# A hybrid attention layer on one core: all first projections in a written order, first tokens without their shift, broadcast conditions, and 26 gate rows in the output projection

## The chip, the core and the metric

One Trainium2 chip; the kernel runs on one core of it. The metric is the device time of one execution in microseconds. The engines are named as in the profile: PE (TensorE, matrix products), DVE (VectorE), ACT (ScalarE), POOL (GpSimd), and SP, which here only issues DMA transfers. POOL can issue transfers too, on a queue of its own.

## The reference

One layer of a diffusion transformer over 512 latent tokens x and 256 context tokens (width 2048, float32), cut to what the first half computes:

```python
mod_x = silu(c) @ w_ada + b_ada          # 6 x 2048: sh1, s1, g1, sh2, s2, g2
mod_c = silu(c_ctx) @ w_ada + b_ada
h  = rmsnorm(x, norm1_w)   * (1 + s1)  + sh1
hc = rmsnorm(ctx, norm1_w) * (1 + s1c) + sh1c
p  = concat(h, hc) @ w_in                # q, k, v of 8 heads; latents c_q, c_kv; rotary key
o_da  = differential attention of 8 heads (two softmax maps each)
o_mla = latent attention of 8 heads (from rmsnorm(c_q), rmsnorm(c_kv))
x  = x + g1 * (concat(o_da, o_mla) @ w_o)
h2 = rmsnorm(x, norm2_w) * (1 + s2) + sh2
x  = rmsnorm(x + g2 * conv_ffn(h2), final_w)
```

sh1 and s1 are needed for both kinds of tokens; of g1, sh2, s2 and g2 only the latent half is used. Since h = u + sh1 with u the scaled and normed token, h @ w = u @ w + sh1 @ w: a shift can be left out of a product and its row of constants added afterwards.

## The kernel before

Tokens lie transposed: kt 0 to 15 are the sixteen pieces of 128 of the width, each 128 partitions by 512 latent (or 256 context) tokens. Every product is split in three: operands are a high float32r part and a low rest, and `mm3` issues high x high, high x low and low x high (L104 to L106). Making the two parts of a weight block is `split`: a copy on ACT (L80) and a subtraction on DVE (L81).

The order of instructions on each engine up to the feed-forward part comes from the framework's scheduler; only in the feed-forward part is it written by hand.

First stage. x and the context are squared and summed for the norm. c and c_ctx are loaded as rows, passed through silu on one partition and spread to all by products with ones (L199) and copies (L200): the tiles cb and ccb. `modulation(u)` makes scale and shift for kts 2u and 2u+1. The scale weights for both kts (adak, 2 MB) go through PE in products with 32 columns of conditions (L219), a copy of the result (row, L221) and a turn that puts it on partitions (L223). The shift weights of one kt (a row of `ada`, 1 MB, in two halves, L244) are multiplied with cb and ccb and summed on DVE for even kts (L251); for odd ones PE transposes them (L258), ACT copies (L259) and PE multiplies (L219). Then tokens: h = x * scale * 1/rms (L330), its high part with the shift (L332, ACT) and its low part (L333, DVE). With the split block of w_g0 (128 x 640) each kt feeds five latent and four context features, 15 matmuls of 512 columns and 12 of 256.

Second stage. ckv norm, keys of heads 0 and 1, query of head 0; features 0 to 6 (two blocks of weights each, `feature`); three features of c_q, without context; two halves of the values, eight blocks each (36 matmuls of 512). The keys, queries and values go to HBM (k_d, q0_d, v_d) as high and low parts. Beside this 48 rows for the gates and the second modulation are computed by `gemv`: a row of 1 MB loaded on SP's queue (L168) and one DVE instruction with an accumulator (L171). `next_gemv` takes the next rows, 32 to 79 here.

Then eight heads of differential attention (`da_head`: keys ks and klz are loaded at L527 and L528, scores at L482; head h's query is a feature computed just ahead), eight latent heads, the output projection (32 blocks, four groups g of eight kb, with 16 gate rows, L704), and the feed-forward part, half of the time.

Of the kernel before, what the change touches and what calls it, by code (L numbers as in the profile page):

```python
# [17 lines left out]
P = 128  # L18
D = 2048
KT = D // P  # L20
T = 512
# [31 lines left out]
def layer_kernel(ctx: ExitStack, tc: tile.TileContext, small, rope, c_row, cc_row, x_t, ctx_t, ada, ada_k,  # L53
# [33 lines left out]
    def wblock(src, cols=1024, pool=None):  # L87
        pool, full = (pool, cols) if pool else (wp, 1024)
        raw = pool.tile([P, full], F32, tag="wr", name=nm("wr"), bufs=3 if full == 1024 else 2)
        nc.sync.dma_start(raw[:, :cols], src)  # L90
        hi = pool.tile([P, full], F32R, tag="wh", name=nm("wh"), bufs=3)
        lo = pool.tile([P, full], F32R, tag="wl", name=nm("wl"), bufs=3)
        split(hi[:, :cols], lo[:, :cols], raw[:, :cols])
        return hi, lo
# [15 lines left out]
    sm.tile([P, 88], F32, name="edge")  # L110
# [55 lines left out]
    def gemv(pool, j, srcs, bufs=2):  # L166
        w = pool.tile([P, D], F32, tag="ada", name=nm("ada"), bufs=bufs)
        nc.sync.dma_start(w, ada[j])  # L168
# [11 lines left out]
    hcp = tc.alloc_tile_pool(name="hcp", bufs=17, side="right")  # L180
# [4 lines left out]
    st = tc.alloc_tile_pool(name="st", bufs=1, reuse_waits="tile")  # L185

    cb = st.tile([P, D], F32, name="cb")
    ccb = st.tile([P, D], F32, name="ccb")  # L190
    cpad = st.tile([P, KT, 32], F32, name="cpad")
    gp.memset(cpad, 0.0)
    sc.activation(cpad[:, :, 0:2], smt[:, OFF["cc"]:OFF["cc"] + 2 * KT].rearrange("p (k i) -> p k i", i=2), AF.Silu)
    for row, wide in ((c_row, cb), (cc_row, ccb)):
        nc.sync.dma_start(wide[0:1], row)
        sc.activation(wide[0:1], wide[0:1], AF.Silu)
        for j in range(0, D, 512):
            t = b_tile()
            pe.matmul(t, ones32[0:1], wide[0:1, j:j + 512], start=True, stop=True)  # L199
            ve.tensor_copy(wide[:, j:j + 512], t)  # L200
    exp_ln_tables()

    sel = sm.tile([P, 2], F32, name="sel")
    ve.tensor_tensor(sel, ident[:, 0:2], ident[:, 32:34], op=ALU.add)
    for j in (64, 96):
        ve.tensor_tensor(sel, sel, ident[:, j:j + 2], op=ALU.add)
    ve.tensor_scalar(out=b1, in0=smt[:, OFF["b_ada"] + 16:OFF["b_ada"] + 32], scalar1=1.0, scalar2=None, op0=ALU.add)


    g0b = [b_tile() for _ in range(4)]  # L210
    acc = g0b[3]

    def products(src, n):


        for j in range(4):
# [1057 lines left out]
```

## Time and profile before

| | us |
|---|---|
| median of 3 runs (lowest, highest) | 2451.57 (2449.83, 2454.16) |
| profiled execution, its own time | 2454.1 |
| its span, first to last instruction | 2451.9 |
| first stage, to the last matmul of the first projection | 0 to 182.9 |
| second stage | 186.7 to 477.9 |
| until the first score of the attention | 495.2 |
| output projection | 893 to 1062 |

The profiled execution lies 2.5 above the median. Times in the traces are from the first instruction on. "Busy" is the time in which an engine works on an instruction; a PE that is busy need not be on the path that sets the end. In rows such as `x48 | 112.8, 2349 | 50.5` the first number behind the bar is the group's busy time in us, the second the mean of one in ns, the third the engine's idle time ahead of them, with what ended it.

### The profile page before, as it was taken

The page shows a single profiled execution, that of the slowest core. Times are in us where ns is not written, and L with a number is a line of the kernel's source. Part 1 is how long each engine was busy: PE and PEld are TensorE (multiplying, and loading weights), DVE is VectorE, ACT ScalarE, POOL GpSimd, SP SyncE. Part 2 cuts the span into 40 slices and gives each one's busy share as a digit, 9 for nine tenths or more (in the row PEclk, how much of TensorE's full clock was granted, in tenths as well). Part 3 has the DMA queues.
Part 4 walks back from the last instruction along what each step waited for, and adds up shares of the span by engine and source line. Part 5 has one row for each costly group of instructions (what it writes and reads, how often), then busy time and mean ns, then how long its engine had stood idle before and what let it go on. Part 6 is the DMA issues. An engine that isn't in the chain of part 4 may idle for free.

```text
span 2451.9 us, 32940 instructions
## 1 busy us (share of the span) xinstructions
PE 2375.5 (97%) x12788; PEld 1988.9 (81%) x12788; DVE 1726.3 (70%) x2272; ACT 1102.5 (45%) x1666; POOL 242.1 (10%) x270
## 2 busy tenths in 40 slices
PE   7999999999999999999999999999999999999997
PEld 3778887877777778888888888888888888888887
DVE  4668785388868877377666666666666666666667
ACT  4342121155545542244545454545454545454553
POOL 0000000122100003100111111111111111111113
PEclk8999999999999999999999999999999999999999
DMA  7868898554411149423555655555555555555572
GB/s 276 283 228 297 321 340 289 189 181 137 141 59 44 44 159 337 152 85 112 134 141 135 141 135 141 134 142 134 140 135 143 133 143 133 144 132 142 133 213 78
DMA packets 130706, 403.31 MB, mean 164 GB/s; under 512 B 14323, under 2 KB 25075, under 8 KB 122099
## 3 DMA queue, kind: packets, MB, share of 16 engines
q1 hardware_dynamic: 104118, 350.87, 43.4%
q0 software_dynamic: 25280, 49.30, 11.5%
q8 instruction: 100, 1.64, 0.3%
q10 hardware_dynamic: 1152, 1.05, 0.1%
q14 instruction: 56, 0.46, 0.1%
HBM read 331.68 MB, written 69.48 MB: 164 GB/s over the span
## 4 chain that ended last, share of the span: by engine, by line
PE 84%; DVE 8%; ACT 3%; DMA 3%; issue 1%; POOL 1%; SPq 0%; DVEq 0%; ACTq 0%; POOLq 0%
PE y L973 12%; PE b L105 10%; PE b L104 10%; PE b L106 10%; PE z L973 6%; PE y L975 6%; PE z L975 3%; PE s L104 3%; PE s L105 3%; PE s L106 3%; PE s L482 3%; PE x L973 2%; DMA ada<-in_ada 2%; PE x L975 1%; PE f L104 1%
## 5 line engine op out<-in xcount | busy, mean ns | idle before, releaser
L104 PE MATMUL b<-ah,wh 128*128 128x512 f32 (+1 forms) x672 | 259.1, 386 | 0.0
L105 PE MATMUL b<-al,wh 128*128 128x512 f32 (+1 forms) x672 | 259.0, 385 | 0.0
L106 PE MATMUL b<-ah,wl 128*128 128x512 f32 (+1 forms) x672 | 258.0, 384 | 0.0
L994 POOL DMA_DIRECT2D x_d<-xs x160 | 139.7, 1003 | 1166.4 <-ACT xs L993 1164.3
L949 DVE TENSOR_TENSOR wl<-wr,wh 128x1024 fp32r<-128x1024 f32 x126 | 153.8, 1221 | 128.7 <-ACT wh L943 128.7
L949 DVE TENSOR_TENSOR wl<-rb,wh 128x1024 fp32r<-128x1024 f32 x124 | 151.2, 1220 | 128.0 <-ACT wh L943 128.0
L80 ACT CAST wh<-wr 128x1024 fp32r<-128x1024 f32 (+3 forms) x118 | 115.9, 982 | 259.0 <-PE b L105 68.3
L943 ACT CAST wh<-wr 128x1024 fp32r<-128x1024 f32 x126 | 132.3, 1050 | 206.3 <-PE b L105 100.7
L943 ACT CAST wh<-rb 128x1024 fp32r<-128x1024 f32 x124 | 130.2, 1051 | 190.0 <-PE b L105 112.5
L949 DVE TENSOR_TENSOR wl<-ws,wh 128x1024 fp32r<-128x1024 f32 x123 | 150.1, 1221 | 88.8 <-ACT wh L943 88.8
L81 DVE TENSOR_TENSOR wl<-wr,wh 128x1024 fp32r<-128x1024 f32 (+3 forms) x118 | 137.3, 1164 | 89.4 <-ACT wh L80 89.0
L171 DVE CUSTOM_DVE_ANT_0 ada<-ada,cb,smt 128x2048 f32<-128x2048 f32 x64 | 151.6, 2369 | 62.4 <-DMA ada<-in_ada 62.1
L943 ACT CAST wh<-ws 128x1024 fp32r<-128x1024 f32 x123 | 128.3, 1043 | 137.0 <-PE b L105 45.2
L106 PEld LDWEIGHTS b<-ah,wl 128*128 128x128 f32 x672 | 126.3, 188 | 25.6
L104 PEld LDWEIGHTS b<-ah,wh 128*128 128x128 f32 x672 | 126.6, 188 | 22.9
L105 PEld LDWEIGHTS b<-al,wh 128*128 128x128 f32 x672 | 126.6, 188 | 22.0
L104 PE MATMUL b<-a2k,wh 128*128 128x512 f32 (+1 forms) x352 | 133.1, 380 | 6.6 <-ACT a2k L756 5.0
L106 PE MATMUL b<-a2k,wl 128*128 128x512 f32 (+1 forms) x352 | 132.5, 376 | 0.0
L973 PE MATMUL y<-b2k,wh 128*128 128x512 f32 x410 | 106.9, 390 | 0.0
L484 DVE TENSOR_REDUCE m<-s 128x1 f32<-128x768 f32 x96 | 90.5, 949 | 15.3 <-PE s L482 14.9
L993 ACT ACTIVATE xs<-b,modx 128x512 f32<-128x512 f32 x160 | 101.0, 680 | 0.5 <-PE y L973 0.3
L973 PEld LDWEIGHTS y<-b2k,wh 128*128 128x128 f32 x410 | 77.0, 188 | 17.1
(471 smaller groups left out, 5937.4 us busy)
## 6 DMA issues: line engine op xcount, KB each, us to landing
ada<-in_ada SPq DMA_DIRECT2D x64, 1024.0 KB, 6.8
rb<-in_w_up SPq DMA_DIRECT2D x123, 512.0 KB, 4.4
wr<-in_w_dn SPq DMA_DIRECT2D x84, 512.0 KB, 4.3
x_d<-xs POOLq DMA_DIRECT2D x160, 256.0 KB, 6.0
wr<-in_w_up SPq DMA_DIRECT2D x53, 512.0 KB, 4.2
wr<-in_w_f SPq DMA_DIRECT2D x34, 512.0 KB, 5.9
adak<-in_ada_k SPq DMA_DIRECT2D x32, 512.0 KB, 6.2
ada<-in_ada SPq DMA_DIRECT2D x32, 512.0 KB, 6.6
```

Of the source, the lines that this page charges most:

```text
L80: sc.copy(dst_h, src)
L81: ve.tensor_tensor(dst_l, src, dst_h.bitcast(F32), op=ALU.subtract)
L104: pe.matmul(out, st[0], mv[0], start=start, stop=False, **kw)
L105: pe.matmul(out, st[0], mv[1], start=False, stop=False, **kw)
L106: pe.matmul(out, st[1], mv[0], start=False, stop=stop, **kw)
L171: ve.tensor_tensor_reduce(out=junk, in0=w, in1=vec, op0=ALU.mult, op1=ALU.add, scale=1.0, scalar=col("b_ada", j), accum_out=dst[:, j:j + 1])
L943: sc.copy(hi, raw)
L949: ve.tensor_tensor(lo, raw, hi.bitcast(F32), op=ALU.subtract)
L973: pe.matmul(o, w[j][0], hs[j], start=start and j == 0, stop=False, skip_group_check=True)
L975: pe.matmul(o[:, h0], w[j][1], hs[j][:, h0], start=False, stop=j == 7, skip_group_check=True)
L993: sc.mul(x, po, modx[:, 80 + dt:81 + dt])
L994: gp.dma_start(x1_d[dt], x, accum_op=ALU.add)
```

## The change

Both stages are written as straight code whose order on all five engines is the order of the program (`manual_schedule`). In words, part by part:

- SP loads x first, then scale weights for three passes, w_g0 and the context. cb and ccb are loaded to all 128 partitions (1 MB each) and passed through silu there; the products and copies that spread them are gone.
- Kts 0 to 7 enter the first projection and the first block of feature 0 without their shift (KA = 8). Shift rows come whole on POOL's queue into two buffers, in the order 8 to 15, 0 to 7, and all are summed on DVE; the transposes are gone. 23 of the 32 sums are ahead of feature 0, nine behind.
- `add_shift` adds the shift to the stored tokens of kts 0 to 7 on DVE and ACT beside the first values; the first half of the values takes its blocks in the order 4 to 7, 0 to 3.
- The row of constants that is missing (shift x w_g0, shift x first block of feature 0) is computed by `bias_products`: those weights are loaded once more on POOL's queue, into the rows' buffers, and multiplied on PE with the shifts padded to 32 columns. `with_bias` adds it on ACT to the outputs of the first projection and of feature 0, when they are used.
- Blocks come in the order: feature 0, values half 0, features 1 to 6 and c_q, values half 1. A block's raw weights have two buffers instead of three, its high and low part are made two blocks ahead (`step`). Keys 0 and 1 and the first query are made beside features 4 and 5, the norms beside feature 6 and the values.
- 64 `gemv` rows: 38 in the second stage on POOL's queue, 26 in the output projection on SP's (5 in group 0, 21 in groups 1 to 3).
- During the last value block the attention's key tiles are allocated, and head 0's keys and queries loaded; the values of the second half are split into twelve free tiles and put out on SP's queue.

The core of the diff:

```diff
+    KA, NU = 8, KT // 2
+    KB = ((4, 5, 6, 7, 0, 1, 2, 3), tuple(range(8)))
...
+    row_order = [*range(KA, KT), *range(KA)]
+    def row_load(kt):
+        rows[kt] = sp_.tile([P, D], F32, tag="ada", name=nm("ada"), bufs=2)
+        gp.dma_start(rows[kt], ada[kt])
+    def row_sums(count, upto=None):
...
+            if i and n_ < KT:
+                row_load(row_order[n_])
+    with tc.manual_schedule(engines=every):
...
+        for u in range(NU):
+            if u + 2 < NU:
+                scale_load(u + 2)
...
+            if u:
+                g0_mm(2 * u, (0, 1))
+            if u + 2 < NU:
+                scale_products(u + 2)
+            if u:
+                g0_mm(2 * u + 1, (0, 1))
+            if u + 1 < NU:
+                next_tokens(u)
+            if u + 2 < NU:
+                row = scale_row(u + 2)
+                scale_turn(u + 2, row)
...
+            elif u < NU - 1:
+                row_sums(3)
...
+    def step(block, *tasks):
+        i = len(steps)
+        block()
+        cast(i + 2)
+        for k, task in enumerate(tasks or [lambda: None]):
+            task()
+            if k == 0:
+                low(i + 2)
+                load(i + 4)
+        steps.append(i)
...
+        step(block(2, 0), feature_keys(1, gemvs(1)))
+        bias_products(0)
+        step(block(2, 1), gemvs(1), gemvs(1))
+        bias_products(1)
+        step(block(3, 0), feature_keys(2, gemvs(1)))
+        bias_products(2)
+        step(block(3, 1), gemvs(1))
+        bias_products(3)
+        bias_rows()
+        step(block(4, 0, bias_turn), feature_keys(3, gemvs(1)))
...
+        step(values(6), gemvs(1), gemvs(1))
+        sp_.release()
+        cbp.release()
+        block_ = values(7)
+        block_()
...
+        for i in range(2):
+            nc.sync.dma_start(qs0[i].bitcast(F32), q0_d[i])
+        keys0 = da_keys(0)
...
-            if g and kb % 4 != 3:
+            if kb != 7 if g else kb > 2:
                 next_gemv(wo, 1)
```

Where instructions now stand, at three places (the first on two engines). In these rows a2k are latent and c2k context tokens, wh and wl a block's high and low part, b_ and s_ tiles of PSUM.

PE inside the first projection, before: transposes of a shift row (ident, ada) and products with the copied result (wt) stand between the matmuls.

```order
L258 MATMUL b_189<-ident,ada_476 128x128 x8
L258 MATMUL b_189<-ident,ada_478 128x128 x4
L104 MATMUL s_428<-a2k_702,wh_472 128x512
L104 MATMUL s_429<-a2k_702,wh_472 128x512
L104 MATMUL b_186<-a2k_702,wh_472 128x512
L258 MATMUL b_189<-ident,ada_478 128x128 x4
L105 MATMUL s_428<-a2k_703,wh_472 128x512
L106 MATMUL s_428<-a2k_702,wl_473 128x512
L104 MATMUL b_187<-c2k_700,wh_472 128x256
L104 MATMUL s_428<-a2k_702,wh_472 128x512
L219 MATMUL b_189<-wt_480,cpad 32x128 x16
```

And now: between the matmuls of two kts only the scale products (adak) and their turn (sel, row).

```order
L285 MATMUL b_263<-adak_487,cpad 32x256 x2
L285 MATMUL b_263<-adak_489,cpad 32x256 x2
L285 MATMUL b_263<-adak_491,cpad 32x256 x2
L285 MATMUL b_263<-adak_493,cpad 32x256 x2
L285 MATMUL b_263<-adak_495,cpad 32x256 x2
L285 MATMUL b_263<-adak_497,cpad 32x256 x2
L285 MATMUL b_263<-adak_499,cpad 32x256 x2
L285 MATMUL b_263<-adak_501,cpad 32x256 x2
L296 MATMUL b_263<-sel,row_548 128x2 x2
L107 MATMUL b_260<-a2k_522,wh_536 128x512
L108 MATMUL b_260<-a2k_523,wh_536 128x512
L109 MATMUL b_260<-a2k_522,wl_537 128x512
```

The rows of L258 and their products are gone from PE; the products of a later pass stand in one piece ahead of the second kt.

DVE in one pass of the first projection, now: the scales of kts 8 and 9 (b_263), their tokens (h_, then the low parts a2k, c2k) and low parts of weights (wl), then the first of three sums over shift rows (a sum is two rows here, the second reads it out).

```order
L302 TENSOR_SCALAR a_91<-b_263,b_92,smt 128x2 x2
L381 SCALAR_TENSOR_TENSOR h_915<-a2k_185,a_91,rinv_269 128x512
L381 SCALAR_TENSOR_TENSOR h_915<-c2k_229,a_91,rinv_270 128x256
L381 SCALAR_TENSOR_TENSOR h_920<-a2k_187,a_91,rinv_269 128x512
L381 SCALAR_TENSOR_TENSOR h_920<-c2k_229,a_91,rinv_270 128x256
L244 SCALAR_TENSOR_TENSOR a2k_914<-h_915,modx,a2k_913 128x512
L244 SCALAR_TENSOR_TENSOR c2k_912<-h_915,modc,c2k_911 128x256
L389 TENSOR_TENSOR wl_928<-wr_837,wh_927 128x640
L244 SCALAR_TENSOR_TENSOR a2k_919<-h_920,modx,a2k_918 128x512
L244 SCALAR_TENSOR_TENSOR c2k_912<-h_920,modc,c2k_911 128x256
L389 TENSOR_TENSOR wl_936<-wr_839,wh_935 128x640
L260 ISA junk_943,modx<-ada_812,cb,smt 128x2048
```

Before, in the same place of the program, half of the rows were summed in pieces of 1024:

```order
L235 TENSOR_SCALAR a_91<-b_189,b_92,smt 128x2 x2
L330 SCALAR_TENSOR_TENSOR h_876<-a2k_220,a_91,rinv 128x512
L330 SCALAR_TENSOR_TENSOR h_912<-a2k_228,a_91,rinv 128x512
L330 SCALAR_TENSOR_TENSOR h_876<-c2k_222,a_91,rinv 128x256
L330 SCALAR_TENSOR_TENSOR h_912<-c2k_222,a_91,rinv 128x256
L251 ISA junk_636,modx<-ada_632,cb,smt 128x1024
L251 ISA modx 128x1
L81 TENSOR_TENSOR wl_645<-wr_642,wh_644 128x640
L251 ISA ada_632,modc<-ada_632,ccb,smt 128x1024
L251 ISA modc 128x1
L251 ISA junk_639,modx<-ada_634,cb,modx 128x1024
L251 ISA modx 128x1
```

What moved to DVE are the rows of the odd kts, and the sums of a row of kts 0 to 7 no longer stand ahead of that kt's tokens.

POOL beside features 1 to 3, now: the gate rows (ada) and the four loads for the missing constants (bw) share one queue.

```order
L171 DMA ada_2131<-in_ada 128x2048
L171 DMA ada_2198<-in_ada 128x2048
L647 MEMSET bias_2207 128x256
L656 DMA bw_2213<-in_w_g 128x640 x3
L171 DMA ada_2274<-in_ada 128x2048
L171 DMA ada_2280<-in_ada 128x2048
L656 DMA bw_2283<-in_w_g 128x640 x3
L171 DMA ada_2357<-in_ada 128x2048
L656 DMA bw_2366<-in_w_g 128x640 x2
L171 DMA ada_2424<-in_ada 128x2048
L664 DMA bw_2430<-in_w_f 128x1024
L171 DMA ada_2512<-in_ada 128x2048
```

Before, POOL's queue had nothing between the start and the second half of the values, where it put them out:

```order
L192 MEMSET cpad 128x512
masks.py:199 ISA
masks.py:199 AFFINE_SELECT ident<-ident 128x128
L470 DMA v_d_137<-kh_3769 128x4x128
L470 DMA v_d_137<-kl_3770 128x4x128
L470 DMA v_d_137<-kh_3775 128x4x128
L470 DMA v_d_137<-kl_3776 128x4x128
L470 DMA v_d_137<-kh_3781 128x4x128
```

The loads of gate rows moved from SP's queue to this one, the value puts from this one to SP's.

PE from the last value matmul into the attention, before: the query of head 1 (f_) stands ahead of the first score (L482).

```order
L105 MATMUL f_4000<-a2k_1599,wh_3765 128x512
L106 MATMUL f_4000<-a2k_1598,wl_3766 128x512
L104 MATMUL f_4000<-a2k_1636,wh_3765 128x512
L105 MATMUL f_4000<-a2k_1637,wh_3765 128x512
L106 MATMUL f_4000<-a2k_1636,wl_3766 128x512
L482 MATMUL s_3833<-ks_3825,qs_3821 128x512
L482 MATMUL s_3833<-klz_3815,qs_3821 128x512
L482 MATMUL s_3833<-ks_3825,qs_3821 128x256
```

Now the scores (L830) follow the last value block (L107 to L109):

```order
L107 MATMUL b_3159<-wh_3471,c2k_1273 128x512
L108 MATMUL b_3159<-wl_3472,c2k_1273 128x512
L109 MATMUL b_3159<-wh_3471,c2k_1274 128x512
L107 MATMUL b_3159<-wh_3471,c2k_1273 128x512
L108 MATMUL b_3159<-wl_3472,c2k_1273 128x512
L109 MATMUL b_3159<-wh_3471,c2k_1274 128x512
L830 MATMUL s_3647<-ks_3588,qs_3584 128x512
L830 MATMUL s_3647<-klz_3578,qs_3584 128x512
L830 MATMUL s_3647<-ks_3588,qs_3584 128x256
L830 MATMUL s_3647<-klz_3578,qs_3584 128x256
L830 MATMUL s_3656<-ks_3588,qs_3585 128x512
L107 MATMUL f_3813<-a2k_350,wh_3519 128x512
```

The query of head 1 has moved behind the first scores.

More of the change, by code (lines that the diff above doesn't have):

```diff
@@ L193, in layer_kernel @@
[L193 to L203, printed above, removed]
@@ L358, in next_block @@
         return wready.pop(0)
[L360 to L367 removed]
+    hx, hc, xs, cs, g0w, rows = [], [], [], [], [], {}
+    sel = sm.tile([P, 2], F32, name="sel")
```

742 lines of the change are left out of this document (496 added, 246 removed).

## Prediction

> **What bounds the kernel now.** I read the page first, then busy time by stretch, then the chain of waits and the groups of the first 190 us. The page (slices of 61 us):
>
> ```profile
> PE 2375.5 (97%) x12788; PEld 1988.9 (81%) x12788; DVE 1726.3 (70%) x2272; ACT 1102.5 (45%) x1666; POOL 242.1 (10%) x270
> ...
> PE   7999999999999999999999999999999999999997
> ...
> PEclk8999999999999999999999999999999999999999
> DMA  7868898554411149423555655555555555555572
> GB/s 276 283 228 297 321 340 289 189 181 137 141 59 44 44 159 337 152 85 112 134 141 135 141 135 141 134 142 134 140 135 143 133 143 133 144 132 142 133 213 78
> ```
>
> TensorE is busy throughout at the full granted clock except in the first slice; DVE (VectorE) has room. So only time in which TensorE idles, or does work that the change takes away, can be won. The stretches (entry; first projection; its end; features and values; way into the attention; output projection, and its part with gate rows):
>
> ```profile
> 0.00:75.20 75.20, 54.93 (x241) 29.82 (x241) 36.32 (x68) 31.65 (x58) 1.15 (x7) 0.91 0.73 264
> 75.20:182.90 107.70, 107.58 (x932) 83.71 (x932) 73.87 (x144) 43.20 (x85) 0.00 (x0) 1.00 0.77 263
> 182.90:186.70 3.80, 1.76 (x5) 0.68 (x4) 3.69 (x8) 2.23 (x4) 0.00 (x0) 1.00 0.03 12
> 186.70:477.90 291.20, 286.58 (x1393) 240.02 (x1394) 205.50 (x236) 62.03 (x78) 0.00 (x0) 0.99 0.81 291
> 477.90:495.20 17.30, 12.45 (x55) 9.96 (x54) 6.20 (x8) 4.99 (x8) 9.10 (x12) 0.92 0.81 278
> 893.00:1062.00 169.00, 168.43 (x734) 137.22 (x732) 93.92 (x86) 44.84 (x53) 29.03 (x27) 1.00 0.69 242
> 926.00:985.00 59.00, 59.00 (x262) 48.87 (x261) 43.73 (x38) 15.10 (x17) 18.00 (x13) 1.00 0.92 337
> ```
>
> TensorE works 55 of the first 75 us, nearly all of the next 108, 287 of 291 in the features, and all of the output projection. The entry and the projection are different cases: in the entry it waits; in the projection it is on the chain, but with shift work that after leaves out. From the chain of waits (start, length), and two places of the timeline of TensorE:
>
> ```profile
> 52.37 1.22 PE s L104 x2
> ...
> 75.20 0.73 PE s L104 x2
> ...
> 96.08 1.86 PE b L219 x32
> ...
> 98.73 0.37 PE b L223 x4
> ```
> ```profile
> 182.71 0.39 PE L106 MATMUL b<-a2k,wl 128*128 128x512 f32 x1
> ...
> 186.74 0.50 PE L104 MATMUL b<-a2k,wh 128*128 128x512 f32 x1 [1.57 <-ACT wh L80]
> ```
> ```profile
> 495.24 0.77 PE L482 MATMUL s<-ks,qs 128*128 128x512 f32 x1 [4.89 <-DMA ks<-k_d]
> ```
>
> Kt 0 starts at 52.37, kt 2 at 75.20, and the 14 kts from 2 to 15 end at 182.9. The second and third fence show the 3.8 us to feature 0, and the first score, which waited 4.89 us for a key transfer.
>
> **The change part by part.** All terms are against this execution: 2454.1 us, 2.5 above the median of the runs (2451.57).
>
> Entry, until kt 2's first matmul (75.2 now). After, x comes first, no shift row stands before kt 0 to 7, and c arrives by broadcast load. What must land before that matmul, from the DMA issues:
>
> ```profile
> x_d<-xs POOLq DMA_DIRECT2D x160, 256.0 KB, 6.0
> ...
> adak<-in_ada_k SPq DMA_DIRECT2D x32, 512.0 KB, 6.2
> ```
>
> One adak load is 512 KB, so a pass of two kts has 2.10 MB. x 4.19 MB (sixteen pieces of x_d's 256 KB) + three passes of adak 6.29 + four w_g0 rows 1.31 + context 2.10 + two broadcasts 2.10 + small 0.3 = 16.3 MB; the two rows that the POOL queue sends at once add some 1.6. At the best rate shown (337 GB/s, 926 to 985) 17.9 MB take 53 us, 3 more to the first landing, 1.9 for the products (row 96.08) that stand ahead of kt 2: 57, so **-18**. Bounds: 50, if the rows don't compete; 66, if 16.3 MB move at the entry's own 264 GB/s. I take the best rate, since the loads are queued without waits between them. Ends: -25 to -9. The products that spread c over partitions, and DVE's copies of them, go from a stretch in which TensorE is idle for 20 us; nothing is booked for them.
>
> First projection, kt 2 to 15. Its rows (75.2 to 182.9; x, mean ns behind the bar), and the pace of matmuls of both widths:
>
> ```profile
> L258 PE MATMUL b<-ident,ada 128*128 128x128 f32 x100 | 15.7, 280 | 0.0
> L259 ACT COPY wt<-b 128x512 f32<-128x512 f32 x26 | 15.2, 585 | 38.1 <-PE b L258 38.0
> ...
> L81 DVE TENSOR_TENSOR wl<-wr,wh 128x640 fp32r<-128x640 f32 x13 | 10.7, 820 | 0.1
> ...
> L333 DVE SCALAR_TENSOR_TENSOR a2k<-h,modx,a2k 128x512 fp32r<-128x512 f32 x14 | 10.5, 750 | 5.1 <-ACT a2k L332 5.1
> ...
> L330 DVE SCALAR_TENSOR_TENSOR h<-a2k,a,rinv 128x512 f32<-128x512 f32 x12 | 8.4, 744 | 0.0
> ...
> L219 PE MATMUL b<-wt,cpad 128*32 128x128 f32 x224 | 7.6, 276 | 0.0
> ...
> L333 DVE SCALAR_TENSOR_TENSOR c2k<-h,modc,c2k 128x256 fp32r<-128x256 f32 x14 | 6.7, 479 | 0.0
> ...
> L330 DVE SCALAR_TENSOR_TENSOR h<-c2k,a,rinv 128x256 f32<-128x256 f32 x12 | 5.2, 478 | 0.0
> ...
> L235 DVE TENSOR_SCALAR a<-b,b,smt 128x2 f32<-128x2 f32 x12 | 2.8, 275 | 8.3 <-PE b L223 8.3
> ```
> ```profile
> 195.80 0.40 PE L104 MATMUL b<-a2k,wh 128*128 128x512 f32 x1
> ...
> 196.85 0.40 PE L104 MATMUL b<-a2k,wh 128*128 128x512 f32 x1
> ```
>
> Six matmuls, three of 512 columns and three of 256, take 1.05 us: a kt with 15 and 12 takes 4.9. TensorE in a pass after: 9.8 + adak products 1.86 + turn 0.37 = 12.0. Gone are the transposes (L258, 15.7), the products with them (L219, 7.6) and the waits on ACT's copies (L259). On DVE a pass has 2 x (0.744 + 0.478 + 0.750 + 0.479 + 0.820) = 6.5 for tokens and low parts, three row sums, and 0.55 for the scales. A row sum and its read of the sum, and DVE's split of a block, from 186.7 to 477.9:
>
> ```profile
> L171 DVE CUSTOM_DVE_ANT_0 ada<-ada,cb,smt 128x2048 f32<-128x2048 f32 x48 | 112.8, 2349 | 50.5 <-DMA ada<-in_ada 50.2
> ...
> L81 DVE TENSOR_TENSOR wl<-wr,wh 128x1024 fp32r<-128x1024 f32 x38 | 46.4, 1221 | 26.9 <-ACT wh L80 26.7
> ...
> L171 DVE DVE_READ_ACCUMULATOR2_ANT modx<- 128x1 f32 x48 | 4.0, 82 | 0.0
> ```
>
> Three sums are 3 x 2.43 = 7.3, so DVE needs 14.4 a pass: it takes TensorE's place as the bound. DMA: 2.10 + 0.66 + 1.5 rows of 1.05 = 4.33 MB, 12.8 us at 337 GB/s. Five passes of 14.4; the sixth has no products, and its sums run beside the seventh, save one that kt 15 needs: 10.2; the seventh 9.8; 1 for the start: 93 against 107.7, **-14.7**. Ends: 87 (12.0 to 12.6 a pass) and 105 (17, second rival): -21 to -3.
>
> Its end. Feature 0's blocks are split beforehand; the norm sums and key work of 182.9 to 186.7 lie later, beside matmuls. 0.5 of 3.8 stays: **-3.3** (-3.8 to 0).
>
> Features and values. The matmuls are the same, and TensorE's 286.6 busy holds the norm sums too. Added on TensorE: correction products, 8 kts of 768 columns, 6144; a pass's adak products are 4096 columns in 1.86, so 2.8; six turns at 0.37 for two, 1.1. Then 290.5, and waits. DVE: 205.5 - 10 rows x 2.43 + the nine row sums left over from the first stage x 2.43 + 8 additions of shifts x (0.744 + 0.750 + 0.478 + 0.479) = 223, and, as an estimate, up to 17 of key and value splits that now stand in the stretches on both sides (where DVE shows 3.7 and 6.2 busy, so this is generous): 240 of 300, covered. The rows' loads, in this stage and in the output projection:
>
> ```profile
> DMA to landing us min/median/max: 4.8/6.8/9.5
> ```
> ```profile
> L171 DVE CUSTOM_DVE_ANT_0 ada<-ada,cb,smt x16: 2340/2352/3384, 901.2 to 984.4; 128x2048 f32<-128x2048 f32 x16
> ```
>
> With two buffers, and each next load behind the row's own sum on POOL's queue, a row comes each (6.8 + 0.75 + 2.43)/2 = 5.0 us (0.75 for issue, nearest row 0.866 below); from the second half of the first values on, four blocks of 8.2 want two rows each, one per 4.1. Two raw buffers for weights instead of three cost nothing while a 512 KB load lands in adak's 6.2 and a block lasts 8.2 or more. A lag of 0.9 x 8 = 7 us lies inside the two blocks (16 us) that are split ahead. It isn't covered where TensorE itself waits for a load behind those rows: the four correction loads use the rows' two buffers and queue. I put 6 us on the first and 4 on the second (a two-row cycle is 10 at most, and DVE's key work ahead of them uses part of it), none on the others, which stand a block later with one row between: 290.5 + 10 = 300.5, **+9**. Ends: 0 (the products fit into today's idle 4.6) and +30 (each of four points waits a full two-row cycle of 10 less 2.5).
>
> Into the attention. Keys and queries of head 0 are loaded during the last value block, so of 477.9 to 495.2 the 4.89 on ks go; head 1's query (part of its 12.45 busy) only moves behind the scores. **-5** (-6, if the 12.45 also run at the full clock instead of 0.92; -2, if the loads are late).
>
> Output projection. 26 rows instead of 16, 21 of them in 24 blocks. 32 blocks in 169.0 are 5.28 each, so a row per 6.0 us is asked; the sixteen rows from 901.2 to 984.4 came one per 5.55, beside a busy TensorE. **+1** (0 to +12).
>
> POOL issues 54 rows and the corrections. What one POOL issue takes now (DVE is busy 70% of the span, by the page):
>
> ```profile
> L994 POOL DMA_DIRECT2D x_d<-xs x160: 850/866/1232, 1194.7 to 2365.2; - x160
> ```
>
> 0.85 to 1.23, below a row's 5: hidden by POOL's empty queue (its next work is the 0-fills and key set-up before the attention). The Trainium skill ("SBUF — State Buffer", Who interferes with whom) speaks against this queue: a DMA issued from GpSimd waits for its descriptors while DVE runs a copy, cast or tensor_scalar in a two-port mode; a row sum is none of these, the nearest here are copies. This case's 160 issues show no such wait; by the rule the sum would rise as in the fifth rival. What is left (order inside the heads, MLA, FFN): 0, within 5.
>
> Sum: -18 - 14.7 - 3.3 + 9 - 5 + 1 = -31: 2423 for this execution, **2420** for the median.
>
> **The rivals.**
> 1. The fourth stage stretches: DVE in its written order comes late with low parts after the corrections. For it: DVE 240 of 300 in strict order, and row waits of 50.2 behind L171 now. Against: two blocks are split ahead. 20 more: 2440.
> 2. The projection waits for adak. Nine buffers hold one pass's eight, so the next eight start after the products (1.86) and then share the DMA with rows: 6.2 to land and 9 for 3 MB behind, 17 a pass. Five passes + 20 = 105: 12 more, 2432. Against: DMA has 13 of 14.4 to do.
> 3. Slower: rows on POOL's queue land late. 42 loads (38 rows, four corrections) through two buffers take 42 x (L + 2.8)/2; with L the time to land they pass 300 + 31 from L = 13 on; the gate rows bind the end, as the pool is released then. At 14 it is 353, and the kernel 2420 + 53 = 2473. For it: POOL's queue needs more engine time per MB:
>
> ```profile
> q1 hardware_dynamic: 104118, 350.87, 43.4%
> q0 software_dynamic: 25280, 49.30, 11.5%
> ```
>
> 0.23% against 0.12% per MB. Against: its transfers are 256 KB and less there, and land in 6.0, below the rows' 6.8 from SP.
> 4. The output projection becomes DMA-bound (share 0.92 with rows now), 10 more: 2430. Against: ten more rows are 31 us of transfers, and 0.31 of 169 is free.
> 5. Each POOL issue waits for the DVE instruction that runs, at most a sum's 2.35: L = 9.2, a row each 6.2. The eight rows in pairs then lag 17, one more than the cover; with the corrections' 2.35 each some 8 more: 2428. It is the mechanism of the skill's sentence above. Against: the issues took 0.87 at the median and 1.23 at most, with DVE at 70% over the span.
>
> **How the numbers follow.** About 0.2% (5 us) is what a measurement of this kernel tells from no change. Forecast 0.52, rivals 0.16, 0.11, 0.09, 0.08, 0.04. Of the first rival 0.03 eats the whole gain. Faster 0.88, same 0.03, slower 0.09. Range 2400 (entry and projection near their good ends, 13 together, and 7 of the features' 9 unneeded) to 2446 (rival 1 with most of 5).
>
> **What would show it.** Kt 0's first matmul near 30, kt 2's near 57; passes of 14 to 15 us with DVE over nine tenths; the last one ends near 150. TensorE waits for the two first correction loads and hardly otherwise; the first score right behind the last value matmul near 451; the output projection still near 169. Wrong: passes of 16 or more, low parts that TensorE waits for, rows landing over 9 us.

## Result, and the profile after

The changed kernel takes 2433.28 us (median of 4 runs, 2429.65 to 2436.97) against 2452.07 beside it: ratio 0.9924, 95% interval 0.9905 to 0.9942, so 19 us less. The forecast was 2420 in 2400 to 2446. The sign and the range held; the gain is three fifths of the forecast 32, and it came about otherwise than the sum said. Two terms were each far off, in opposite directions, and both lie outside the ends given for them. That the total still lies in the range is in part luck.

The page of the profile after (its span is 2430.2, so 21.7 below the span before; slices of 61 us):

```profile
PE 2332.7 (96%) x12408; PEld 1962.5 (81%) x12408; DVE 1779.8 (73%) x2305; ACT 1102.3 (45%) x1660; POOL 273.2 (11%) x324
...
PE   5989799999999999989999999999999999999997
...
PEclk9999899999999999999999999999999999999999
DMA  9865877854411159723546555555555555555572
```

The first slice now moves more, and a dip stands in TensorE's fifth slice, where the kernel before had none. Busy time by stretch (entry to kt 2; first projection; features and values; to the first score; output projection):

```profile
0.00:55.50 55.50, 31.08 (x174) 19.40 (x175) 31.49 (x65) 27.32 (x48) 2.65 (x10) 0.91 0.93 352
55.50:138.60 83.10, 81.46 (x561) 66.84 (x561) 78.85 (x109) 28.41 (x47) 5.27 (x10) 1.00 0.80 282
138.60:464.10 325.50, 300.79 (x1467) 248.46 (x1465) 240.11 (x296) 85.81 (x126) 30.79 (x57) 0.96 0.73 257
464.10:466.00 1.90, 0.38 (x3) 0.04 (x1) 1.64 (x3) 0.70 (x2) 0.00 (x0) 1.00 1.06 239
874.00:1042.00 168.00, 167.43 (x732) 137.02 (x731) 119.04 (x106) 45.00 (x53) 32.65 (x27) 1.00 0.82 306
```

Kt 2 starts at 55.5 instead of 75.2, the first projection ends at 138.6 instead of 182.9: 44 us are won there. The third row is the reader's main one: 325.5 us, to the start of the last value matmul, for a stage that took 293.1 before (186.7 to 479.8, where the last value matmul starts there, and not to the 477.9 that the prediction took as the end). TensorE is busy in 300.8 of them at a mean clock of 0.96. What it waited for between 100 and 300:

```profile
PE s L107 <- DVE kl L81: 7.8, 1, 7.8
PE b L109 <- DVE wl L213: 7.2, 1, 7.2
PE b L660 <- DVE a L1064: 6.7, 1, 6.7
PE b L108 <- DVE wl L213: 2.5, 1, 2.5
```

Four waits, 24 us, and each has a place. The 7.2 is feature 0's first block: its low part stands behind five row sums in DVE's written order.

```profile
131.94 0.82 DVE L389 TENSOR_TENSOR wl<-wr,wh 128x640 fp32r<-128x640 f32 x1
132.69 2.34 DVE L260 CUSTOM_DVE_ANT_0 junk<-ada,cb,smt 128x2048 bf16<-128x2048 f32 x1
...
135.07 2.35 DVE L260 CUSTOM_DVE_ANT_0 ada<-ada,ccb,smt 128x2048 f32<-128x2048 f32 x1
...
137.35 2.35 DVE L260 CUSTOM_DVE_ANT_0 junk<-ada,cb,smt 128x2048 bf16<-128x2048 f32 x1
...
139.74 2.35 DVE L260 CUSTOM_DVE_ANT_0 ada<-ada,ccb,smt 128x2048 f32<-128x2048 f32 x1
...
142.70 2.35 DVE L260 CUSTOM_DVE_ANT_0 junk<-ada,cb,smt 128x2048 bf16<-128x2048 f32 x1 [0.60 <-DMA ada<-in_ada]
...
144.98 1.22 DVE L213 TENSOR_TENSOR wl<-wr,wh 128x1024 fp32r<-128x1024 f32 x1
```

TensorE had finished the first projection at 138.7 and could go on at 146.2. The 2.5 is the same at 197, behind additions of shifts. The 7.8 (at 250) is a PSUM tile that isn't free, because the splits of the first half of the values wait for tiles that are still being put out; the 6.7 (at 268) is the first correction product, whose padded shifts (the copies `bias`) and weights stand behind these splits, the keys of feature 1 and two row sums. (The tile `a` that the wait names is a small unrelated operation, the last one on DVE ahead of the product.)

```profile
252.26 0.69 DVE L81 TENSOR_TENSOR kl<-s,kh 128x512 fp32r<-128x512 f32 x1 [5.06 <-DMA v_d<-kl]
...
257.48 0.69 DVE L81 TENSOR_TENSOR kl<-s,kh 128x512 fp32r<-128x512 f32 x1 [4.40 <-DMA v_d<-kl]
...
274.92 0.17 DVE L649 COPY bias<-modx 128x8 f32<-128x8 f32 x1
```

**What a long wait costs on top.** TensorE's busy time and granted clock (the last but two columns) around the first wait:

```profile
131.00:138.60 7.60, 7.60 (x45) 6.66 (x44) 7.43 (x8) 2.54 (x4) 1.06 (x2) 1.00 0.63 217
142.00:146.20 4.20, 0.00 (x0) 0.00 (x0) 3.60 (x6) 1.50 (x4) 0.53 (x1) 0.72 0.60 193
146.20:149.20 3.00, 2.94 (x7) 2.39 (x8) 3.00 (x4) 0.00 (x0) 0.43 (x1) 0.50 0.77 259
149.20:152.20 3.00, 3.00 (x11) 2.36 (x11) 3.00 (x4) 1.05 (x1) 0.09 (x1) 0.75 0.69 229
152.20:155.00 2.80, 2.80 (x20) 2.55 (x19) 2.80 (x3) 0.00 (x0) 0.53 (x1) 1.00 0.81 316
```

After 7 idle us TensorE runs at half clock for 3 us and regains the full clock by 152. Between 146.2 and 152.2 that is 0.5 x 3 + 0.25 x 3 = 2.3 us of clock lost. The Trainium skill ("TensorE: Matmul & The Clock Gate", What's actually happening) says that the throttled clock is the default state and that some 3.4 us of sustained work releases it; the trace agrees, with 3 to 6. The prediction had no term for this.

Where the 32 us of the longer stage are: the four waits 24, half clock behind the three long ones 3 x 2.3 = 7, the correction products about 8 (starts to starts), less the one wait of 4.6 and its half clock (0.50 and 0.52 for 3 us each, so 2.9) that the kernel before had here. That makes 31 to 32; about 1 of it is counted twice, since the first correction products run at half clock.

### The profile page after: what moved, and what is told of

It reads as the page before. It is cut to its first block, busy times and chain, and to the rows that moved or that the text cites. A ratio compares the mean times of both kernels' runs of the same rounds, so it can differ in the third digit from the quotient of the medians.

```text
span 2430.2 us, 32271 instructions
## 1 busy us (share of the span) xinstructions
PE 2332.7 (96%) x12408; PEld 1962.5 (81%) x12408; DVE 1779.8 (73%) x2305; ACT 1102.3 (45%) x1660; POOL 273.2 (11%) x324
## 4 chain that ended last, share of the span: by engine, by line
PE 78%; DVE 8%; issue 7%; DMA 3%; ACT 3%; POOL 1%; SPq 0%; DVEq 0%; POOLq 0%; ACTq 0%
PE y L1314 12%; PE b L108 9%; PE b L107 9%; PE b L109 9%; PE z L1314 6%; PE y L1316 6%; PE z L1316 3%; PE s L830 3%; PE x L1314 2%; PE s L108 2%; PE s L109 2%; PE s L107 2%; PE f L107 1%; PE x L1316 1%; PE pt L842 1%
## 5 line engine op out<-in xcount | busy, mean ns | idle before, releaser
L107 PE MATMUL b<-ah,wh 128*128 128x512 f32 (+1 forms) x672 | 259.1, 386 | 0.0
L109 PE MATMUL b<-ah,wl 128*128 128x512 f32 (+1 forms) x672 | 258.0, 384 | 0.0
L1284 ACT CAST wh<-wr 128x1024 fp32r<-128x1024 f32 x126 | 132.3, 1050 | 206.1 <-PE b L108 100.4
L109 PEld LDWEIGHTS b<-ah,wl 128*128 128x128 f32 x672 | 126.3, 188 | 25.6
L107 PEld LDWEIGHTS b<-ah,wh 128*128 128x128 f32 x672 | 126.6, 188 | 23.0
L107 PE MATMUL b<-a2k,wh 128*128 128x512 f32 (+1 forms) x352 | 136.5, 390 | 7.1 <-ACT a2k L1097 5.1
L109 PE MATMUL b<-a2k,wl 128*128 128x512 f32 (+1 forms) x352 | 134.3, 382 | 7.2 <-DVE wl L213 7.2
L80 ACT CAST wh<-wr 128x1024 fp32r<-128x1024 f32 (+2 forms) x64 | 64.3, 1005 | 135.0 <-PE b L108 42.9
L210 ACT CAST wh<-wr 128x1024 fp32r<-128x1024 f32 x38 | 39.9, 1049 | 141.5 <-PE s L108 46.1
L81 DVE TENSOR_TENSOR wl<-wr,wh 128x1024 fp32r<-128x1024 f32 (+2 forms) x64 | 78.3, 1223 | 32.3 <-ACT wh L80 31.9
```

What stands on the lines that cost most here:

```text
L81: ve.tensor_tensor(dst_l, src, dst_h.bitcast(F32), op=ALU.subtract)
L107: pe.matmul(out, st[0], mv[0], start=start, stop=False, **kw)
L109: pe.matmul(out, st[1], mv[0], start=False, stop=stop, **kw)
L1284: sc.copy(hi, raw)
```

## Experiments

All kernels but one start from the changed one and are compared by ratio to the kernel before, run beside them on the same chip. Times in the table are from each trace; "last row" is the start of the last gate row of the stage on DVE. In the kernel before, and in the one made from it, the query of head 1 stands ahead of the first score, so their first scores don't compare with the others'.

| | median us | ratio (95%) | last row | last value matmul | first score |
|---|---|---|---|---|---|
| kernel before | | 1 | 446.6 | 479.8 | 495.2 |
| changed kernel | 2433.3 | 0.9924 (0.9905 to 0.9942) | 455.9 | 464.1 | 466.0 |
| low parts first | 2438.1 | 0.9948 (0.9931 to 0.9966) | 459.9 | 466.6 | 469.8 |
| third pair of put tiles | 2437.2 | 0.9938 (0.9919 to 0.9958) | 459.1 | 467.2 | 468.8 |
| constants early | 2435.6 | 0.9928 (0.9911 to 0.9946) | 455.2 | 463.9 | 465.0 |
| these three | 2433.3 | 0.9929 (0.9905 to 0.9953) | 457.3 | 466.2 | 467.1 |
| seven rows later | 2434.6 | 0.9940 (0.9925 to 0.9955) | 454.2 | 453.6 | 464.3 |
| rows later and the three | 2437.6 | 0.9959 (0.9943 to 0.9976) | 454.0 | 453.0 | 466.0 |
| puts of 2 KB | 2433.0 | 0.9933 (0.9918 to 0.9947) | 453.7 | 462.8 | 463.8 |
| 16 gate rows at the end | 2471.1 | 1.0084 (1.0065 to 1.0102) | 486.6 | 483.9 | 496.3 |
| rows spaced | 2429.9 | 0.9920 (0.9903 to 0.9936) | 437.8 | 459.1 | 459.4 |
| spaced, and order | 2419.5 | 0.9883 (0.9867 to 0.9899) | 434.4 | 456.0 | 456.2 |
| before, 26 rows | 2447.2 | 0.9992 (0.9983 to 1.0002) | 392.6 | 474.3 | 489.5 |
| kts 0 to 3 unshifted | 2434.9 | 0.9945 (0.9924 to 0.9966) | 452.4 | 462.0 | 464.3 |

### Taking the waits away one by one

Low parts first:

```diff
                 for i in range(2):
                     cast(i)
-                    row_sums(2)
                     low(i)
                     load(i + 2)
-                row_sums(1)
+                row_sums(5)
...
+        early = i < 10
+        if early:
+            low(i + 2)
+            load(i + 4)
         for k, task in enumerate(tasks or [lambda: None]):
             task()
-            if k == 0:
+            if k == 0 and not early:
```

> Base: the changed kernel (span 2430.2, median 2433.3), in which TensorE waits 7.4 us for the low part of feature 0's first block and 2.7 for one of the first values, both behind row sums or shift additions in DVE's written order, and runs 4 to 5 us at half clock behind the long wait. Here the low parts of the first twelve blocks stand ahead of the sums of their step. Theory A (each wait is only a matter of order and is worth itself plus about 2.2 of half clock): both waits fall to under 2.5 together, last value matmul 10 earlier, median near 2423. Theory B (DVE is full until the shifts are added at 207, so what is not waited for here is waited for at the next low part): less than 4 gained, 2430.

```profile
PE b L663 <- DVE a L1067: 10.7, 1, 10.7
PE s L107 <- DVE kl L81: 8.7, 1, 8.7
PE b L107 <- ACT wh L210: 2.8, 1, 2.8
PE b L108 <- DVE wl L213: 2.0, 4, 0.8
```

The wait at 139 fell to 1.5 and the values began 7 us earlier (157.9 instead of 164.7), but the wait for the PSUM tile grew to 8.7 and the one for the constants to 10.7. The last value matmul came no earlier (466.6 instead of 464.1). Theory B's outcome, at other places than it named.

Third pair of put tiles:

```diff
-            return [lambda t=t: put_value(0, v0, t) for t in ts]
+            return [lambda t=t, k=k: put_value(0, v0, t, [rtmp(F32R), rtmp(F32R)] if k % 3 == 2 else None)
+                    for k, t in enumerate(ts)]
```

> Base: the changed kernel, in which TensorE waits 8.0 us ahead of feature 2's context half for a PSUM tile, while the splits of the first half of the values wait on DVE for their two pairs of tiles to be put out (5.1 and 4.4 us on v_d<-kl). Here every third put uses the two free tiles of the rotary work, so three pairs rotate. Theory A: the 8.0 and the half clock behind it (2.2) go, and the wait of 6.9 for the constants, which stands behind the same splits on DVE, shrinks by 3 or more: 11 to 14 less, median near 2420. Theory B (the puts land as slowly whatever the tile, because 512-byte pieces share the DMA with rows and weights): the wait only moves to the next pair or to the keys, 3 less, 2430.

```profile
PE b L660 <- DVE a L1065: 15.6, 1, 15.6
```

The wait of 7.8 is gone, and the next one has grown from 6.7 to 15.6: theory B again.

Constants early (padding behind the first half of the values, first load one step earlier):

```diff
+        bias_prep()
         step(block(1, 0), a, b, gemvs(1), c)
...
+        bias_load(0)
         step(block(2, 0), feature_keys(1, gemvs(1)))
         bias_products(0)
```

> Base: the changed kernel, in which TensorE waits 6.9 us for the first correction product. Here the shifts are padded (two copies on DVE) right behind the first half of the values, and the first correction load stands one step earlier on POOL's queue; products stay where they are. Theory A (the wait is for the two DVE copies and for a load that stand behind splits and a row sum): the 6.9 and the half clock behind it go, 9 less, median near 2424. Theory B (what is late is the transfer itself, behind the rows that share two buffers): the gate rows come later instead, or the second load waits: 2 less, 2431.

The wait went from 6.7 on DVE to 5.0 on the transfer of the weights, and the stage ended where it did (463.9). All three together:

> All three edits at once on the changed kernel. Theory A: the gains add, 10 + 10 + 9 = 29 less, median near 2404, stage from feature 0 to the last value matmul near 297 instead of 325. Theory B (DVE's total of 240 and the rows' cycle of 5 us are the limit, and waits only move): less than half of it, 2420 or more.

Theory A is refuted: 466.2, with waits of 7.3 and 8.0 between 246 and 272. What is saved before 246 is lost in the same 40 us.

### Is it the transfers?

The changed kernel's windows show a trough and a burst (the last two columns are the DMA share and GB/s):

```profile
180.00:190.00 10.00, 10.00 (x46) 8.29 (x45) 6.35 (x11) 4.21 (x7) 0.00 (x0) 1.00 0.24 83
190.00:200.00 10.00, 7.70 (x34) 6.03 (x33) 6.68 (x12) 3.91 (x6) 0.00 (x0) 1.00 0.00 0
200.00:210.00 10.00, 9.76 (x43) 7.96 (x44) 7.26 (x11) 3.42 (x5) 0.00 (x0) 1.00 0.23 64
210.00:290.00 80.00, 65.00 (x316) 52.63 (x315) 54.15 (x74) 12.68 (x17) 10.94 (x21) 0.89 0.90 308
```

From 180 to 210 hardly anything moves: DVE adds shifts, no row is asked for beyond the two that lie ready, and the next weights wait for buffers. Then puts, rows, corrections and weights come at once. Seven rows moved out of the burst, to seven steps from feature 5 to the second value block:

```diff
-                [gemvs(1), gemvs(1)], [gemvs(1), gemvs(1)], [gemvs(1), gemvs(1)], [gemvs(1), gemvs(1)])
+                [gemvs(1)], [gemvs(1)], [gemvs(1)], [gemvs(1)])
...
-        step(block(1, 1), d, gemvs(1), e_, f_, gemvs(1))
+        step(block(1, 1), d, e_, f_)
...
-        step(values(1), gemvs(1))
+        step(values(1), gemvs(1), gemvs(1))
```

> Base: the changed kernel. Its DMA is idle from 185 to 205 and busy 0.83 to 1.00 from 210 to 290, where twelve gate rows, the puts of the first half of the values, 3.1 MB of correction weights and the split blocks' weights fall together. Here seven gate rows move from that stretch to steps between features 5 and the second value block (38 rows in all as before). Theory C (that burst of DMA is the bound until 290, the waits of 8.0 and 6.9 are where TensorE meets it): 7 MB less are 20 us of DMA, both waits shrink to under 4 together, stage 12 to 15 shorter, median near 2420. Theory D (the two pairs of put tiles and DVE's written order set these waits, whatever the DMA does): within 3 us of 2433.

> The three edits of order (low parts first, third pair of put tiles, constants early) and the seven rows moved later, together. Theory C: what the three edits of order won before 210 is no longer given back at 246 to 290: 20 to 25 less than the changed kernel, median near 2411. Theory D: as with the three alone, 2433.

Theory C was right about TensorE: both waits are gone, and the last value matmul is at 453.6 and 453.0 instead of 464.1. A row that moves takes its sum on DVE with it, but DVE was busy in only 54 of the 80 us from 210 to 290, and it is the transfers that changed: the puts of the first half of the values land in 4.9 us at the median instead of 8.3. Theory C's times are refuted: the first kernel is no faster, and the second looks slower than the changed kernel (its interval begins just above the end of the other). In the second of these, the first score:

```profile
465.96 0.77 PE L848 MATMUL s<-ks,qs 128*128 128x512 f32 x1 [9.89 <-DMA ks<-k_d]
```

Now TensorE waits 9.9 us for the keys of head 0. They can be loaded only when the rows' buffers are given up, behind the last row. The first fence has the last rows of the changed kernel, the second those of the kernel with rows later and the three edits, and the third the loads that start in it when its last sum ends (454.0 + 2.35):

```profile
L174 DVE CUSTOM_DVE_ANT_0 ada<-ada,cb,smt x38: 2339/2350/2355, 208.3 to 455.9; 128x2048 f32<-128x2048 f32 x38
```
```profile
L174 DVE CUSTOM_DVE_ANT_0 ada<-ada,cb,smt x38: 2343/2351/2355, 210.1 to 454.0; 128x2048 f32<-128x2048 f32 x38
```
```profile
456.48 0.80 SPq L826 DMA_DIRECT2D qs<-q_d  x2
457.33 0.68 SPq L817 DMA_DIRECT2D ks<-k_d  x1
```

The last row starts at 455.9 in the changed kernel and at 454.0 here, though TensorE is 11 us ahead. What this kernel loses, its trace shows behind the first score, which stands at 466.0 in both: to the first result of the output projection it takes 442.8 us instead of 438.5, and behind the wait the mean granted clock is 0.82 from 464 to 480 and 0.91 from 480 to 500, where the changed kernel's is 1.00.

Pieces of 512 bytes were not the point:

```diff
-    v_d = [dram.tile([4, P, 2, NKEY, P], F32, name=f"v_d{i}") for i in range(2)]
+    v_d = [dram.tile([P, 2, NKEY, 4 * P], F32, name=f"v_d{i}") for i in range(2)]
...
-            nc.sync.dma_start(v_d[half][:, :, i, t].rearrange("h p d -> p h d"), g.bitcast(F32))
+            nc.sync.dma_start(v_d[half][:, i, t], g.bitcast(F32))
```

> Only the layout of the values in HBM differs: a put writes 2 KB per partition in one piece instead of four of 512 bytes, and each head's load reads pieces of 512 bytes instead of 6 KB. Theory C with small pieces as the main part of the burst: the puts land in 5 to 6 us instead of 8 to 9, the wait of 8.0 falls below 4, the stage is 5 to 8 shorter, and the heads, with DMA to spare, lose nothing: near 2427. Theory D': pieces don't matter beside the rows, 2433; if the heads' loads of small pieces are late, slower by some us in the heads.

```profile
PE b L660 <- DVE a L1064: 10.0, 1, 10.0
...
PE s L107 <- DVE kl L81: 2.3, 1, 2.3
```

The wait of 7.8 fell to 2.3, the one behind it grew to 10.0; no gain.

### Is it the chain of rows?

One part undone, ten rows more in this stage, one in each of ten steps:

```diff
-            if kb != 7 if g else kb > 2:
+            if g and kb % 4 != 3:
...
-        step(block(3, 1), gemvs(1))
+        step(block(3, 1), gemvs(1), gemvs(1))
```

> One part undone: 16 gate rows in the output projection as before the change, 48 in the features and values; the ten more stand one each in ten steps from feature 3 to the fourth value block. Theory C (the burst to 290 binds, behind it the DMA has room at 0.55 to 0.9): 10 MB fall behind the burst; DVE gets 24 more, rows come at 5.0 each for 48 in 300, so the stage is 0 to 6 longer and the output projection the same: 2433 to 2439. Rival: the rows' cycle through two buffers is the bound of the stage: ten more rows are 50 us of cycle, of which 20 or more show: 2453 or more.

```profile
L174 DVE CUSTOM_DVE_ANT_0 ada<-ada,cb,smt x48: 2341/2351/2355, 209.8 to 486.6; 128x2048 f32<-128x2048 f32 x48
```

The rival's outcome: the last row moves by 30.7, the first score by 30.3, the kernel by 38. So, in this order, the 26 rows in the output projection are what lets the rest of the change pay at all. On the kernel before, alone, they are worth nothing that can be told:

```diff
-            next_gemv(kv, 1 if (half * 8 + kb) % 3 else 2)
+            next_gemv(kv, 1 if half * 8 + kb < 11 else 0)
...
-            if g and kb % 4 != 3:
+            if kb != 7 if g else kb > 2:
```

> One part alone on the kernel before: 26 gate rows in the output projection and 38 in the stage ahead, in the new order of rows, nothing else. In the kernel before the last row started at 446.6 and the first score at 495.2, so rows don't end that stage. Theory E: within 3 us of 2450. Rival (rows are a load on DVE and DMA that costs wherever they stand): 5 or more faster.

The ratio is 0.9992, its interval 0.9983 to 1.0002: theory E's "within 3 us". The profiled execution is 4.1 shorter, with the wait at 410 gone; whether 2 us of that are real stays open.

Then 35 rows spread evenly over the stage (one or two a step beside the first values and features 4 to 6, one in six of the eight last value blocks), 29 in the output projection:

```diff
-        step(values(6), gemvs(1), gemvs(1))
+        step(values(6), gemvs(1))
...
-            if kb != 7 if g else kb > 2:
+            if g or kb > 2:
```

> Base: the changed kernel. In every variant with 38 rows so far the last gate row on DVE started between 453.7 and 459.9, whatever TensorE did, and the first score stood 8 to 12 us behind it, since the head's keys can only be loaded when the rows' buffers are given up. Theory E: the rows' chain from 208 on (two buffers, few rows asked beside features 2 to 6, two a block in the last values) is what ends the stage. Here, as the only change, 35 rows are spread evenly over it, the last one in the seventh of the eight last value blocks, and 29 stand in the output projection. Theory E: last row before 445, last value matmul near 454 (the two waits at 250 to 275 go, as with the rows moved later), first score within 2 us of it, output projection within 2 of 168: median near 2422. Rival F (the keys' transfer is late by itself, or three more rows make the output projection wait): 2430 or more.

```profile
459.37 0.39 PE L830 MATMUL s<-ks,qs 128*128 128x512 f32 x1
```
```profile
L174 DVE CUSTOM_DVE_ANT_0 ada<-ada,cb,smt x35: 2341/2349/2353, 208.5 to 437.8; 128x2048 f32<-128x2048 f32 x35
```

The mechanism is as theory E says: the last row is at 437.8, and the first score waits for nothing. The size isn't: two waits fell to 4.3 and one of 5.1 for norm squares on ACT came at 338, so the values end at 459.1 instead of 454; from the first score to the first result of the output projection 441.8 us pass instead of 438.5, and to its last a further 1.2. Of 6.6 us at the first score 2.2 are left at the end of the trace, and the ratio can't be told from the changed kernel's. The trace shows one place: from 650 to 700, where the latent heads begin, the mean granted clock is 0.86, in the changed kernel's trace 1.00. Why, and whether other runs have it, stays open. With the edits of order, and both additions of a shift ahead of their roundings:

```diff
-            for hl, m, n_ in ((hx[kt], modx, T), (hc[kt], modc, C)):
-                t = rtmp()[:, :n_]
+            both = [(hl, m, rtmp()[:, :n_]) for hl, m, n_ in ((hx[kt], modx, T), (hc[kt], modc, C))]
+            for hl, m, t in both:
                 ve.tensor_tensor(t, hl[0].bitcast(F32), hl[1].bitcast(F32), op=ALU.add)
                 high(hl, t, m[:, kt:kt + 1])
+            for hl, m, t in both:
                 rest(hl, t, m[:, kt:kt + 1])
```

> The rows spread as in the run before, and the edits of order with them: low parts first, third pair of put tiles, constants early, and the two additions of a shift ahead of both roundings, so that DVE doesn't wait for ACT in each (11 us of such waits in the changed kernel). Theory E: with the rows out of the way the waits at 139 and 197 count at last: last value matmul near 446, first score right behind, median near 2413. Rival: they are again given back at later low parts, 2422.

```profile
PE b L109 <- DVE wl L213: 5.3, 2, 3.5
PE s L575 <- ACT nq L567: 5.1, 1, 5.1
PE b L678 <- DVE rt L153: 4.8, 1, 4.8
```

This is the fastest kernel: 0.9883 (0.9867 to 0.9899), an interval wholly below the changed kernel's, some 10 us below it. Theory E's 2413 was too low, and its 446 for the last value matmul came out as 456: half of the gain that it named is there by the ratio, two thirds by the medians, so the rival's 2422 is as near. Waits of up to 3.5, 4.8 and 5.1 us are left, one of them for low parts.

### How much to leave unshifted

```diff
-    KA, NU = 8, KT // 2
+    KA, NU = 4, KT // 2
```

> One size changed on the changed kernel: kts 0 to 3 enter without their shift instead of 0 to 7, so four shift rows more must be summed ahead of their tokens; corrections are half (5.5 instead of 8 kts' work on TensorE), four additions of shifts go. In the changed kernel the passes took 13.0, of which DVE's instructions fill nearly all (a row sum follows the next at 2.37, other instructions overlap by 0.08). Theory G (DVE sets the pass): four sums a pass make it 15.3, five such passes 11 longer, and the pass of kts 4 and 5 starts some 9 later, since their rows land after c: first projection ends near 158 instead of 138.5. The rows' chain then starts some 13 earlier (28 of work in DVE's additions halved), last row near 445, TensorE's chain 8 to 12 shorter behind: last value matmul 464 to 472, median 2430 to 2441. Rival H (TensorE's 12.0 and transfers set the pass, DVE has slack): the first projection ends by 145 and the kernel is 8 faster, 2425.

Waits of TensorE, and the first and last start of the scale products (five passes) here and in the changed kernel:

```profile
PE b L285 <- DVE a L302: 10.0, 4, 3.0
```
```profile
L285 PE MATMUL b<-adak,cpad x160: 379/379/634, 61.0 to 129.8; 128*32 128x256 f32 x160
```
```profile
L285 PE MATMUL b<-adak,cpad x160: 379/379/403, 60.6 to 113.2; 128*32 128x256 f32 x160
...
  DVE a L302: 1.6, 3
```

Theory G holds, DVE sets the pass, though a pass was forecast at 15.3. From the first to the last products there are 68.8 us instead of 52.6, four passes of 16.8 (less the 1.6 of the products themselves) instead of 12.8; the projection ends at 157.3 instead of 138.7. And 19 us more in the first stage cost nothing that can be told at the end: the last row starts at 452.4 (445 was forecast), the first score at 464.3. That fits an end of this stage that the first projection doesn't set. It isn't proof, as the additions and corrections behind the projection are halved too: the wait of 7.8 is gone, and the 6.7 has become 3.4.

## Why the prediction came out as it did

| term | forecast | measured |
|---|---|---|
| entry, to kt 2 | -18 | -19.7 |
| first projection, kts 2 to 15 | -14.7 | -24.6 |
| its end, to feature 0 | -3.3 | -3.8 |
| features and values | +9 | +32.4 |
| into the attention, with the heads | -5 | -3.5 |
| output projection | +1 | -0.1 |
| the rest | 0 | -2.4 |
| sum | -31 | -21.7 |

The output projection is taken here from its first result on DVE to its last, and what lies ahead of the first with the heads.

Entry: right in size. The first 55.5 us moved 352 GB/s, above the 337 that the sum took as the best. (Its lower end of 50 should have been 53: 16.3 MB at 337 GB/s are 48.4, and the same 3 and 1.9 follow.)

First projection: right in mechanism, wrong in size. DVE is the bound (78.9 busy of 83.1), but the step added durations, 14.4 a pass, where the distance from start to start is what counts: in the DVE rows above, the low part that starts at 131.94 takes 0.82 and the next instruction starts 0.75 later. Passes took 12.3 to 13.0, and the 83.1 lie below even the lower end of 87.

Features and values: here the step failed. It took DVE's total (forecast 240, measured 240.1) against a stage of 300, called that covered, and looked for waits at the corrections alone: 6 and 4. The first correction waited 6.7, the second hardly, but three more waits stood where the total can't show them, in the order: five sums ahead of the low part that TensorE needed next, the shift additions, and the splits behind their own puts. Low parts that TensorE waits for were one of the prediction's own signs of being wrong. The products with their turns took about 8 instead of 3.9: a product of 512 columns is two rows of the trace and took 0.54 from start to start on average (16 rows, 4.33, some of them at half clock), where the adak products' price gave 0.23, and those of 128 columns with w_g0 took 0.21 (16 rows, 1.68) instead of 0.06. So that price doesn't carry over to these products; why, no run here shows. Half clock had no term.

The third rival was the nearest to what binds the end: "the gate rows bind the end, as the pool is released then". Its break-even was set wrongly. It let 42 loads run through the whole stage of 331 us; but the first gate row is summed at 208, since DVE has shifts to do until then, and 38 rows take until 456, one per 6.7. So no load has to land late (they landed in 5.6 at the median, below the 6.8 from SP before) for the rows to be at the limit; the sixteen-row run has them beyond it, and is slower than the kernel before.

The fifth rival isn't seen. POOL's issues of gate rows beside a DVE that is busy three quarters of the time:

```profile
L171 POOL DMA_DIRECT2D ada<-in_ada x38: 527/528/536, 170.7 to 449.7; - x38
...
DMA to landing us min/median/max: 4.8/5.6/9.0
```

The longest took 0.54. By the Trainium skill's rule that the prediction cites ("SBUF — State Buffer", Who interferes with whom) an issue could have waited for a copy, cast or tensor_scalar on DVE; the trace shows no issue that did, beside sums and two-input operations for the most part. The fourth rival fell too: the output projection took 168.0 with 26 rows at a DMA share of 0.82. The second was wrong: no pass from kt 2 on waited for adak; the scale products' idle of 1.6 us in all was for DVE.

So where did the expected gain go? The first written stage gave 44 us at 138.6 (48 at feature 0), and 16 were left at the last value matmul. About 24 went into waits of which each could be removed, and then reappeared elsewhere; as far as the experiments show, since a burst of transfers to 290 and behind it the rows' chain with the keys' load stood at the same height. Only the kernel that moved rows and order at once got 10 us of it back.

## What to carry to other kernels

When a stage has three chains of nearly the same length (here the matmuls, the row loads through two buffers, and a load that needs their memory), shorten the end of each on paper before booking a gain in one; and look for the moment from which a chain can start, not only for its rate. An engine with a total well under the stage still makes others wait if its order is fixed: put what the next engine needs ahead of what only has to be done some time. Add up starts to starts, not durations, for an engine whose instructions overlap.

## What was not expected of the hardware

A wait of 7 us on TensorE cost 2.3 more at half clock, and behind the wait of 2.5 at 197 the clock stayed at 1.00. DVE's neighbouring instructions overlap by about 0.07 us each, 10% of a 128 x 512 operation.
